# First block's attention: PE's order laid down by the source, scores of both heads in turns and two steps ahead

## The chip, the cores and the metric

The kernel runs on one core of one Trainium2 chip. The metric is the time of one execution on the device, in microseconds (us); of several runs the median is given. The profile is of one execution.

The engines of the core are called as the profile calls them: PE (TensorE; its matmuls, with PEld for the weight loads that run beside them), DVE (VectorE), ACT (ScalarE), POOL (GpSimd) and SP (SyncE, which issues most of the DMAs). Each engine takes its instructions in the order in which they stand in its own list, and waits in front of one until the semaphores that it names have been raised.

## The reference

A chain of three blocks, each on a sequence of 1024 rows of width 1024 in float32. The change is in the first. Its attention is a stick-breaking attention: no softmax over a row, but a running sum along the keys from the right.

```python
def stick_breaking_attention(q, k, v):
    scale = ATT_HEAD_DIM ** -0.5
    outs = []
    for blk in range(S // Q_BLOCK):          # Q_BLOCK = 128
        q0, q1 = blk * Q_BLOCK, (blk + 1) * Q_BLOCK
        z = einsum('bthd,bshd->bhts', q[:, q0:q1], k[:, :q1]) * scale
        log_fail = where(causal, log_sigmoid(-z), 0.0)
        later = cumsum(log_fail, axis=3, reverse=True) - log_fail
        w = where(causal, exp(log_sigmoid(z) + later), 0.0)
        outs.append(einsum('bhts,bshd->bthd', w, v[:, :q1]))
```

There are 8 heads of width 64 and 8 query blocks. The same block also has a gate for each of its two branches (`g_att`, `g_conv`, dense projections of the input), and a branch with a convolution of 31 taps and a layer norm. The second and third blocks follow with an average-pooling mixer, a banded attention, and a state-space layer.

## The kernel before

Dense products are made in three matmuls: each operand is split into a high and a low part, and hi·hi, hi·lo and lo·hi are added up (`mm3`, L156). Half of an output tile, 128 x 512, takes 8 blocks of depth x 3 = 24 matmuls; this text calls it a half dense. The split of a weight is a cast by ACT (`whi`, L146) and a subtraction by POOL (`wlo`, L147).

The attention of the first block walks over four pairs of heads, p = 0 to 3. The two heads of a pair lie in the same tiles `qh, ql, kh, kl`, head 0 in rows 0 to 63, head 1 in rows 64 to 127. For each pair there are eight steps, one for each query block tb (ascending for p = 0 to 2, descending for p = 3). A step, `attention_step`, does for each head:

- scores: three matmuls (qh·kh, qh·kl, ql·kh, L754) per bank `aux`, of which there are two; up to 512 keys make one part, more keys two parts; on the diagonal block a mask is added by a fourth matmul of 128 columns (L756); ACT copies the bank to `z` (L757)
- the chain on `z` and `e`: a minimum on DVE (L758), exponential and logarithm on ACT (L218), a maximum (L761), a scan from the right (L762) and a subtraction (L763) on DVE, an exponential on ACT (L218)
- transposes: pieces of 128 x 128 (L770), up to four to a bank `tp`, of which there are two; a step with more than four blocks (tb of 4 or more) needs two pieces for each head; a copy of each piece to `wt`, by ACT for head 0 (L773) and by DVE for head 1 (L775)

and then for both heads together the values (L783): per key block one matmul for each head, into one bank `o`, which four steps share; after the fourth, DVE multiplies the bank by a gate (`zt`, L707).

Between the steps the source calls the dense work that fills PE: gates after steps 1, 2, 3 and 6, the projections of the next pair's k and q after steps 4 and 5. Each piece of the convolution branch (`conv_branch`, 28 pieces, `K.bg`) is called behind a half dense, two at a time (`K.rate = 2`).

None of this is the order in which the engines run. A scheduler lays each engine's list by the dependences and by priority: the steps stand inside `high_priority(offset=2000)`, so an instruction of a step comes as soon as its operands may be there by the scheduler's estimate, and the dense work falls into the rest. Where `K.after(a, b)` is called, a stands behind b on its engine, without a semaphore.

## Time and profile before

| | |
|---|---|
| median of 3 runs | 3230.51 us (3230.08 to 3234.98) |
| the profiled execution | 3232.07 us |
| its span, from the first to the last instruction | 3230.3 us |
| mean granted TensorE clock | 0.978 |
| busy share of the span | PE 96%, PEld 77%, DVE 64%, POOL 43%, ACT 38% |
| the chain of work that ended last | PE 32%, of it 24% dense (L156); DVE 8%; DMA 3% |

"Busy" is the time in which an engine had an instruction under way. Matmuls overlap at their ends, so the durations of single ones add up to more than the time that passes; the distance from start to start is the cost. A row of the timeline shows the start, the time to the end of the last one of the row, and in brackets how long the engine had stood idle before it and what ended that. The clock is the share of full speed that was granted.

### The profile page before, as it was taken

The page shows a single profiled execution, that of the slowest core. Times are in us where ns is not written, and L with a number is a line of the kernel's source. Part 1 is how long each engine was busy: PE and PEld are TensorE (multiplying, and loading weights), DVE is VectorE, ACT ScalarE, POOL GpSimd, SP SyncE. Part 2 cuts the span into 40 slices and gives each one's busy share as a digit, 9 for nine tenths or more (in the row PEclk, how much of TensorE's full clock was granted, in tenths as well). Part 3 has the DMA queues.
Part 4 walks back from the last instruction along what each step waited for, and adds up shares of the span by engine and source line. Part 5 has one row for each costly group of instructions (what it writes and reads, how often), then busy time and mean ns, then how long its engine had stood idle before and what let it go on. Part 6 is the DMA issues. An engine that isn't in the chain of part 4 may idle for free. (4 is left out here: it accounts for less than half of the span.)

```text
span 3230.3 us, 41367 instructions
## 1 busy us (share of the span) xinstructions
PE 3106.3 (96%) x15397; PEld 2479.5 (77%) x15401; DVE 2052.8 (64%) x3302; ACT 1215.6 (38%) x2294; POOL 1376.0 (43%) x1065
## 2 busy tenths in 40 slices
PE   9999999999989999999999999999989989989997
PEld 7877677778777888777777777778778778778886
DVE  8986886663685364232268767784886887663444
ACT  3025555563252111111144344441114655743443
POOL 2323332214645344777744322342213553474455
PEclk9999999999989999999999999999999999989998
DMA  4132222134321112222212111337344232375322
GB/s 130 52 108 79 72 68 80 46 125 134 124 63 49 57 53 66 70 76 75 66 56 63 46 34 37 122 127 198 97 142 136 92 104 66 124 237 180 118 91 98
DMA packets 159737, 303.92 MB, mean 94 GB/s; under 512 B 23840, under 2 KB 66864, under 8 KB 159536
## 3 DMA queue, kind: packets, MB, share of 16 engines
q1 hardware_dynamic: 149104, 294.96, 28.8%
q10 hardware_dynamic: 10368, 6.30, 0.9%
q8 instruction: 121, 1.98, 0.3%
q14 instruction: 80, 0.66, 0.1%
q0 software_dynamic: 64, 0.03, 0.0%
HBM read 236.59 MB, written 64.62 MB: 93 GB/s over the span
## 5 line engine op out<-in xcount | busy, mean ns | idle before, releaser
L147 POOL TENSOR_TENSOR wlo<-wraw,whi 128x1024 fp32r<-128x1024 f32 (+1 forms) x305 | 750.6, 2462 | 1086.9 <-ACT whi L146 1049.4
L146 ACT CAST whi<-wraw 128x1024 fp32r<-128x1024 f32 (+1 forms) x309 | 308.2, 998 | 795.1 <-PE mm L156 588.7
L568 DVE SCALAR_TENSOR_TENSOR co<-cpad,conv_w,co 128x1024 f32<-128x1024 f32 x120 | 179.7, 1537 | 0.9
L1640 DVE SCALAR_TENSOR_TENSOR h<-cp,conv_w,h 128x512 f32<-128x512 f32 x96 | 90.6, 943 | 20.0 <-ACT h L1638 19.0
L156 PE MATMUL mm<-mixh,whi 128*128 128x512 f32 x256 | 99.3, 393 | 2.9 <-DVE h L927 2.0
L156 PE MATMUL mm<-mixh,wlo 128*128 128x512 f32 x256 | 99.8, 391 | 0.0
L156 PE MATMUL mm<-mixl,whi 128*128 128x512 f32 x256 | 99.7, 391 | 0.0
L218 ACT ACTIVATE e<-e 128x128 f32<-128x128 f32 (+7 forms) x128 | 84.5, 681 | 33.5 <-DVE e L758 32.6
L762 DVE TENSOR_TENSOR_SCAN e<-e 128x128 f32<-128x128 f32 (+7 forms) x64 | 93.9, 1475 | 0.7
L927 DVE TENSOR_TENSOR h<-h,mm 128x512 f32<-128x512 f32 x64 | 43.3, 680 | 59.4 <-PE mm L156 59.3
L761 DVE TENSOR_TENSOR e<-e,z 128x128 f32<-128x128 f32 (+7 forms) x64 | 53.8, 850 | 37.1 <-ACT e L218 37.0
L320 DVE TENSOR_TENSOR sq<-sq,sq 128x512 f32<-128x512 f32 (+1 forms) x46 | 53.8, 1170 | 29.7 <-ACT sq L319 28.7
L218 ACT ACTIVATE z<-z 128x128 f32<-128x128 f32 (+7 forms) x64 | 43.3, 683 | 76.6 <-DVE z L763 76.5
L1958 DVE TENSOR_TENSOR h<-h,mm 128x512 f32<-128x512 f32 x32 | 21.9, 685 | 78.3 <-PE mm L156 78.3
L832 DVE TENSOR_TENSOR sz<-mm,row 128x512 f32<-128x512 f32 x32 | 22.0, 689 | 75.1 <-PE mm L156 75.1
L319 ACT ACTIVATE sq<-h 128x512 f32<-128x512 f32 x60 | 37.7, 629 | 73.4 <-POOL h L1990 29.7
L156 PE MATMUL mm<-y00h,whi 128*128 128x512 f32 x146 | 59.7, 410 | 3.9 <-DVE zt L1797 3.2
L916 DVE TENSOR_TENSOR cv<-mm,cv 128x512 f32<-128x512 f32 x16 | 11.1, 692 | 81.4 <-PE mm L156 81.4
L156 PE MATMUL mm<-y01h,whi 128*128 128x512 f32 x146 | 58.7, 403 | 3.3 <-ACT y01h L68 2.5
L156 PEld LDWEIGHTS mm<-mixh,whi 128*128 128x128 f32 x256 | 48.0, 188 | 15.5 <-issue 3.1
L156 PE MATMUL mm<-y30l,whi 128*128 128x512 f32 x146 | 58.0, 397 | 2.0 <-DVE y30l L71 2.0
L156 PE MATMUL mm<-y01l,whi 128*128 128x512 f32 x146 | 59.2, 406 | 0.2 <-DVE y01l L71 0.2
(1433 smaller groups left out, 10229.1 us busy)
## 6 DMA issues: line engine op xcount, KB each, us to landing
wraw<-w_in SPq DMA_DIRECT2D x76, 512.0 KB, 3.7
wraw<-w_in_even SPq DMA_DIRECT2D x53, 512.0 KB, 3.6
wraw<-w_in_odd SPq DMA_DIRECT2D x22, 512.0 KB, 3.6
sp_g<-gt SPq DMA_DIRECT2D x32, 256.0 KB, 2.0
g<-sp_g SPq DMA_DIRECT2D x32, 256.0 KB, 3.3
wraw<-w_out SPq DMA_DIRECT2D x16, 512.0 KB, 3.5
wraw<-w_out_even SPq DMA_DIRECT2D x32, 256.0 KB, 2.6
wraw<-w_out_odd SPq DMA_DIRECT2D x16, 512.0 KB, 3.6
```

The source lines that it names most:

```text
L146: self.nc.scalar.copy(hi, src)
L147: (eng or self.nc.gpsimd).tensor_sub(lo, src, hi.bitcast(F32))
L156: ins = self.nc.tensor.matmul(ps, a[:, k, :], b[:, cols], start=first and n == 0, stop=last and n == total - 1).ins
L218: ins = self.nc.scalar.activation(out, in_, func, **kw).ins
L319: nc.scalar.activation(sq, src, AF.Square, scale=scale)
L320: (nc.vector if self.count > 5 else self.engines[i]).tensor_add(self.accs[i], self.accs[i], sq)
L568: nc.vector.scalar_tensor_tensor(o, cpad[:, tap:tap + S], cw[:, j, tap:tap + 1], o, op0=ALU.mult, op1=ALU.add)
L761: nc.vector.tensor_tensor(e[:, :L], e[:, :L], z[:, :L], op=ALU.max)
L762: nc.vector.tensor_tensor_scan(e[:, rev], e[:, rev], e[:, rev], 0.0, op0=ALU.add, op1=ALU.bypass)
L832: nc.vector.tensor_mul(t, ps, row[hf])
L927: nc.vector.tensor_add(h[e][:, half(hf)], h[e][:, half(hf)], ps)
L1640: nc.vector.scalar_tensor_tensor(oh, c(d), cw[:, ch, 3 - d:4 - d], oh, op0=ALU.mult, op1=ALU.add)
```

## The change

`attention_step` becomes a class, `Attention1`, with the step cut in four: `open` (its tiles), `scores(s, part)`, `turn` (the transposes) and `values_of`. Steps are numbered through, s = 8p + n. Its parts are called in this order around the dense work: values of step s - 1, transposes of step s, first part of the scores of step s + 2, then a half dense. The second part of the scores comes between two half denses, or, where a step has one half dense only, in the middle of it (`K.within`, behind block 3 of 8). The dense work is handed out by halves: for p < 3 one half each of the next k and q after steps 0 to 3, a whole gate after steps 4 to 7; for p = 3 one half of a gate after each step.

The scores of the two heads take turns (kh·qh of head 0, of head 1, then the next product). The transposes of the two heads take turns by pieces. `K.queue` ties each of these PE instructions, and each dense matmul from then on, behind the one queued before it: PE's order in this stage is that of the source. At the start, the scores of steps 0 and 1 stand behind half 0 of k and q, and half 1 of both behind these.

The operations, their operands and shapes are the same in both kernels.

```diff
@@ mm3
-                ins = self.nc.tensor.matmul(ps, a[:, k, :], b[:, cols], ...).ins
+                ins = self.queue(self.nc.tensor.matmul(ps, a[:, k, :], b[:, cols], ...)).ins
...
+            if self.within and k == x.n // 2 - 1:
+                self.within, step = None, self.within
+                step()
@@
+    def queue(self, step):
+        if self.queued:
+            if self.tail is not None:
+                self.after(step.ins, self.tail)
+            self.tail = step.ins
+        return step
@@ attention of the first block
-    project("k", 0)
-    project("q", 0)
+    steps = Attention1(K, pb, v, mask, qk)
+    (k0, k1), (q0, q1) = by_halves(lambda: project("k", 0)), by_halves(lambda: project("q", 0))
+    k0()
+    q0()
+    K.queued = True
+    with K.tc.high_priority(offset=2000):
+        for s in range(2):
+            steps.open(s)
+            steps.scores(s, 0)
+    k1()
+    q1()
     K.bg += conv_branch(K, pb)
...
+        fill = []
         if p < 3:
-            fill[4] = lambda: project("k", p + 1)
-            fill[5] = lambda: project("q", p + 1)
+            fill += [[r] for name in "kq" for r in by_halves(lambda name=name: project(name, p + 1))]
+        gates = [r for i in range(4) for r in by_halves(lambda i=i: gate(4 * p + i))]
+        fill += [gates[2 * i:2 * i + 2] for i in range(4)] if p < 3 else [[r] for r in gates]
         for n in range(8):
+            s = 8 * p + n
             with K.tc.high_priority(offset=2000):
-                o = attention_step(K, pb, p, tb, qh, ql, kh, kl, v, mask, o if n % 4 else None)
...
-            if n in fill:
-                fill[n]()
+                steps.values_of(s - 1)
+                steps.turn(s)
+                if s + 2 < 32:
+                    steps.open(s + 2)
+                    steps.scores(s + 2, 0)
+            def more(s=s):
+                with K.tc.high_priority(offset=2000):
+                    steps.scores(s + 2, 1)
+            if s + 2 < 32 and len(fill[n]) == 1:
+                K.within = more
+            fill[n][0]()
+            if len(fill[n]) == 2:
+                more()
+                fill[n][1]()
+    K.queued, K.tail = False, None
+    steps.values_of(31)
     K.drain()
@@ class Attention1, scores
+        banks = [K.aux_bank() for _ in range(2)]
+        for i, (a, b) in enumerate(((qh, kh), (qh, kl), (ql, kh))):
+            for hh, ps in enumerate(banks):
+                rows = slice(hh * 64, hh * 64 + 64)
+                K.queue(nc.tensor.matmul(ps[:, :n], a[rows, ts], b[rows, c0:c0 + n], ...))
+        if diag:
+            for ps in banks:
+                K.queue(nc.tensor.matmul(ps[:, n - 128:n], K.identb, self.mask, start=False, stop=True))
@@ class Attention1, turn
         for s0 in range(0, tb + 1, 4):
             ns = min(4, tb + 1 - s0)
+            for hh, (z, wt) in enumerate(zip(zs, wts)):
+                pt = K.tp_bank()
+                for i in range(ns):
+                    K.queue(nc.tensor.transpose(pt[:, i * 128:(i + 1) * 128], z[:, ...], K.ident))
```

Lines move: the dense matmul from L156 to L157, the scores from L754 to L807, the mask from L756 to L810, the copy to `z` from L757 to L812, minimum, maximum, scan and subtraction from L758, L761, L762, L763 to L816, L819, L820, L821, the transposes from L770 to L834, the copies to `wt` from L773 and L775 to L837 and L839, the values from L783 to L853, `zt` from L707 to L859, ACT's exponentials from L218 to L222.

Three places follow, all in the third pair of heads (p = 2), around the steps tb = 4 to 6, as the engines' lists have them. In brackets stands what an instruction waits for: a semaphore of PE, of ACT (Activation), of DVE, of POOL or of a DMA queue. Numbers behind a name tell tiles apart.

PE before, at the scores of step tb = 6: `aux_759` is the second part of head 0, with the mask, and `aux_765` the first part of head 1.

```order
L754 MATMUL aux_759_4831<-kh_573_3735,qh_596_3875 128x384 [waits PE_49]
L754 MATMUL aux_759_4831<-kl_574_3736,qh_596_3875 128x384
L754 MATMUL aux_759_4831<-kh_573_3735,ql_597_3876 128x384
L756 LDWEIGHTS identb_239
L756 MATMUL aux_759_4831<-attmaskb_241,identb_239 128x128
L754 MATMUL aux_765_4858<-kh_573_3735,qh_596_3875 128x512 [waits Activation_49]
L754 MATMUL aux_765_4858<-kl_574_3736,qh_596_3875 128x512
L754 MATMUL aux_765_4858<-kh_573_3735,ql_597_3876 128x512
L156 MATMUL mm_707_4519<-x01l_25_189,whi_702_4485 128x512
L156 MATMUL mm_707_4519<-x01h_24_188,wlo_703_4486 128x512
```

PE after, at the same step: `aux_729` is the first part of head 0, `aux_730` that of head 1.

```order
L807 MATMUL aux_729_4594<-kh_505_3335,qh_543_3522 128x512
L807 MATMUL aux_730_4595<-kh_505_3335,qh_543_3522 128x512
L807 MATMUL aux_729_4594<-kl_506_3336,qh_543_3522 128x512
L807 MATMUL aux_730_4595<-kl_506_3336,qh_543_3522 128x512
L807 MATMUL aux_729_4594<-kh_505_3335,ql_544_3523 128x512
L807 MATMUL aux_730_4595<-kh_505_3335,ql_544_3523 128x512
L157 MATMUL mm_734_4610<-x00h_8_130,whi_732_4605 128x512
L157 MATMUL mm_734_4610<-x00l_9_131,whi_732_4605 128x512
L157 MATMUL mm_734_4610<-x00h_8_130,wlo_733_4606 128x512 [waits Pool_49]
```

Before, the three matmuls of one head's bank stand together; after, those of the two heads take turns, ahead of the dense work.

PE before, at the transposes of step tb = 4, head 1 (`z_716`): one piece of four blocks into `tp_721`, one of a single block into `tp_722`.

```order
L754 MATMUL aux_743_4722<-kh_573_3735,qh_596_3875 128x384 [waits Activation_49]
L754 MATMUL aux_743_4722<-kl_574_3736,qh_596_3875 128x384
L770 MATMUL tp_721_4598<-ident_235,z_716_4577 128x128 [waits Activation_49]
L770 MATMUL tp_721_4598<-ident_235,z_716_4577 128x128 x3
L770 MATMUL tp_722_4604<-ident_235,z_716_4577 128x128
L754 MATMUL aux_743_4722<-kh_573_3735,ql_597_3876 128x384
L756 LDWEIGHTS identb_239
L756 MATMUL aux_743_4722<-attmaskb_241,identb_239 128x128
L156 MATMUL mm_704_4490<-x20l_13_146,whi_702_4485 128x512
```

PE after, at the transposes of the same step (`z_688` is head 0, `z_689` head 1).

```order
L853 MATMUL mm_671_4303<-wt_703_4474,v_242 64x128
L853 MATMUL mm_671_4303<-wt_704_4475,v_242 64x128
L834 MATMUL tp_721_4572<-ident_235,z_688_4391 128x128 [waits PE_49,Activation_49]
L834 MATMUL tp_721_4572<-ident_235,z_688_4391 128x128 x3
L834 MATMUL tp_722_4578<-ident_235,z_689_4392 128x128 [waits PE_49,Activation_49]
L834 MATMUL tp_722_4578<-ident_235,z_689_4392 128x128 x3
L834 MATMUL tp_723_4584<-ident_235,z_688_4391 128x128 [waits Activation_49]
L834 MATMUL tp_724_4587<-ident_235,z_689_4392 128x128 [waits DVE_49]
```

Before, the two pieces of a head stand between scores, with one wait; after, the four pieces of both heads stand behind the values of the step before, the first two waiting for `z` (ACT) and their banks, the third for ACT, the fourth for DVE.

DVE before, in the same stretch: `wt_720` takes head 1 of step tb = 4, `e_734` and `e_741` are the two heads of step tb = 5.

```order
L758 TENSOR_SCALAR e_734_4685<-z_733_4684 128x768 [waits Activation_49]
L761 TENSOR_TENSOR e_734_4685<-e_734_4685,z_733_4684 128x768 [waits Activation_49]
L762 SCALAR_TENSOR_TENSOR e_734_4685<-e_734_4685 128x768 [waits DVE_49]
L763 TENSOR_TENSOR z_733_4684<-z_733_4684,e_734_4685 128x768 [waits DVE_49]
L775 COPY wt_720_4597<-tp_721_4598 128x512 [waits PE_49]
L775 COPY wt_720_4597<-tp_722_4604 128x128 [waits PE_49]
L758 TENSOR_SCALAR e_741_4716<-z_740_4715 128x768 [waits Activation_49]
L761 TENSOR_TENSOR e_741_4716<-e_741_4716,z_740_4715 128x768 [waits Activation_49]
L762 SCALAR_TENSOR_TENSOR e_741_4716<-e_741_4716 128x768 [waits DVE_49]
```

DVE after: `wt_720` is again head 1 of step tb = 4, `e_709` and `e_710` the two heads of step tb = 5, `zt_717` the product with the bank of values of steps tb = 0 to 3.

```order
L816 TENSOR_SCALAR e_709_4490<-z_707_4488 128x768 [waits Activation_49]
L816 TENSOR_SCALAR e_710_4491<-z_708_4489 128x768 [waits Activation_49]
L819 TENSOR_TENSOR e_709_4490<-e_709_4490,z_707_4488 128x768 [waits Activation_49]
L859 TENSOR_TENSOR zt_717_4565<-mm_671_4303,zt_717_4565 128x512 [waits DMAHW7_49,DMAHW1_49,PE_49]
L820 SCALAR_TENSOR_TENSOR e_709_4490<-e_709_4490 128x768 [waits DVE_49]
L839 COPY wt_720_4571<-tp_722_4578 128x512 [waits PE_49]
L819 TENSOR_TENSOR e_710_4491<-e_710_4491,z_708_4489 128x768 [waits Activation_49]
L821 TENSOR_TENSOR z_707_4488<-z_707_4488,e_709_4490 128x768 [waits DVE_49]
L839 COPY wt_720_4571<-tp_724_4587 128x128 [waits PE_49]
L820 SCALAR_TENSOR_TENSOR e_710_4491<-e_710_4491 128x768 [waits DVE_49]
```

Before, both copies to `wt_720` stand together between the chains of two heads; after, the first stands behind the product with `zt` and a scan, and the second behind a maximum and a subtraction more.

## Rows read from the trace of the kernel before

**Rows 1.** Stretches of the stage, all engines: the stretch and its length, busy time of each engine (x instructions), the mean granted clock, the share of the DMA engines and what they moved.

```profile
264.00:370.00 106.00, 98.94 (x537) 73.95 (x538) 91.33 (x137) 62.41 (x118) 35.33 (x28) 0.95 0.19 61
370.00:480.00 110.00, 102.80 (x542) 76.25 (x537) 95.69 (x132) 60.36 (x116) 37.03 (x28) 0.97 0.24 81
480.00:600.00 120.00, 120.00 (x657) 91.10 (x657) 84.68 (x111) 66.89 (x118) 36.51 (x26) 1.00 0.20 67
600.00:712.00 112.00, 110.09 (x599) 81.98 (x598) 71.24 (x90) 67.42 (x118) 18.09 (x7) 0.94 0.24 85
264.00:712.00 448.00, 431.82 (x2326) 323.27 (x2326) 342.93 (x468) 257.08 (x469) 126.97 (x88) 0.97 0.22 73
```

The busy times are in the order PE, PEld, DVE, ACT, POOL.

**Rows 2.** The same stretch, PE alone and one line of the kernel at a time, in this order: scores (L754), masks (L756), transposes (L770), values (L783). Busy time (x instructions), clock, DMA.

```profile
264.00:712.00 448.00, 75.26 (x288) 0.97 0.22 73
...
264.00:712.00 448.00, 14.89 (x64) 0.97 0.22 73
...
264.00:712.00 448.00, 44.05 (x288) 0.97 0.22 73
...
264.00:712.00 448.00, 50.72 (x576) 0.97 0.22 73
```

**Rows 3.** PE's timeline at the scores of a step of the first pair, two banks of 512 columns: start, us, line, operation, tiles and shapes.

```profile
338.80 0.50 PE L754 MATMUL aux<-kh,qh 64*128 64x512 f32 x1
339.14 0.39 PE L754 MATMUL aux<-kl,qh 64*128 64x512 f32 x1
339.37 0.39 PE L754 MATMUL aux<-kh,ql 64*128 64x512 f32 x1
...
340.38 0.23 PE L756 MATMUL aux<-attmaskb,identb 128*128 128x128 bf16 x1
340.42 0.48 PE L156 MATMUL mm<-x20h,whi 128*128 128x512 f32 x1
```

**Rows 4.** PE's timeline in the attention of the second block, where heads in the lower and the upper 64 rows alternate.

```profile
1788.15 0.38 PE L1082 MATMUL aux<-kh,qh 64*128 64x256 f32 x1
1788.16 0.38 PE L1082 MATMUL stat<-kh,ql 64*128 64x256 f32 x1
1788.37 0.28 PE L1082 MATMUL aux<-kl,qh 64*128 64x256 f32 x1
1788.38 0.28 PE L1082 MATMUL stat<-kh,qh 64*128 64x256 f32 x1
1788.49 0.28 PE L1082 MATMUL aux<-kh,ql 64*128 64x256 f32 x1
```

**Rows 5.** PE's timeline at five of its stops in the stage; in brackets the idle time before and what ended it.

```profile
268.93 0.44 PE L754 MATMUL aux<-kh,qh 64*128 64x384 f32 x1 [1.87 <-ACT z L757]
...
350.88 0.76 PE L281 MATMUL stat<-ones,sq 128*128 128x1 f32 x4 [2.86 <-DVE sq L324]
...
352.08 0.63 PE L156 MATMUL mm<-x21h,wlo 128*128 128x512 f32 x1
352.51 0.63 PE L156 MATMUL mm<-x31h,whi 128*128 128x512 f32 x1
...
450.37 0.50 PE L754 MATMUL aux<-kh,qh 64*128 64x512 f32 x1 [2.07 <-ACT z L757]
...
457.05 1.52 PE L783 MATMUL mm<-wt,v 128*64 128x128 f32 x22 [1.36 <-DVE wt L775]
458.51 0.76 PE L770 MATMUL tp<-ident,z 128*128 128x128 f32 x5
...
473.77 2.59 PE L783 MATMUL mm<-wt,v 128*64 128x128 f32 x24 [3.13 <-DVE wt L775]
```

**Rows 6.** Groups of DVE's instructions from 242 to 712 us, by shape: xcount, busy time, mean ns of one, idle time before and what ended it.

```profile
L648 DVE RECIPROCAL lnsum<-lnsum 128x256 f32<-128x256 f32 x16 | 27.9, 1744 | 0.3
...
L762 DVE TENSOR_TENSOR_SCAN e<-e 128x768 f32<-128x768 f32 x8 | 17.2, 2147 | 0.1
...
L775 DVE COPY wt<-tp 128x512 f32<-128x512 f32 x24 | 16.0, 682 | 8.9 <-PE tp L770 8.9
...
L761 DVE TENSOR_TENSOR e<-e,z 128x768 f32<-128x768 f32 x8 | 8.0, 997 | 7.8 <-ACT e L218 7.8
...
L758 DVE TENSOR_SCALAR e<-z 128x768 f32<-128x768 f32 x8 | 5.0, 619 | 2.3 <-ACT z L757 2.3
L707 DVE TENSOR_TENSOR zt<-mm,zt 128x512 f32<-128x512 f32 x7 | 4.6, 664 | 7.3 <-PE mm L783 7.3
```

**Rows 7.** Groups of ACT's instructions from 242 to 712 us, by shape.

```profile
L757 ACT COPY z<-aux 128x512 f32<-128x512 f32 x32 | 18.0, 586 | 6.4 <-PE aux L756 4.7 <-PE aux L754 1.7
L218 ACT ACTIVATE e<-e 128x1024 f32<-128x1024 f32 x16 | 16.9, 1058 | 8.1 <-DVE e L758 8.0
...
L773 ACT COPY wt<-tp 128x512 f32<-128x512 f32 x24 | 13.6, 581 | 6.1 <-PE tp L770 5.9
```

**Rows 8.** The timelines of ACT and POOL where half 0 of q of the first pair is split.

```profile
258.26 0.69 ACT L673 ACTIVATE qkf<-mm,b 128x512 f32<-128x512 f32 x1 [3.38 <-PE mm L156]
258.99 0.62 ACT L146 CAST qh<-qkf 128x512 fp32r<-128x512 f32 x1
...
259.69 1.28 POOL L147 TENSOR_TENSOR ql<-qkf,qh 128x512 fp32r<-128x512 f32 x1 [2.33 <-ACT qh L146]
```

More of the change, by code (lines that the diff above doesn't have):

```diff
@@ L155, in mm3 @@
             for a, b in ((hi, xh), (hi, xl), (lo, xh)):
-                ins = self.nc.tensor.matmul(ps, a[:, k, :], b[:, cols], start=first and n == 0, stop=last and n == total - 1).ins
+                ins = self.queue(self.nc.tensor.matmul(ps, a[:, k, :], b[:, cols], start=first and n == 0, stop=last and n == total - 1)).ins
                 if self.pin is not None:
@@ L667, in project, with ev @@
         qk[name, p] = (hi, lo)
-        def ev(_, hf, ps):
+        def ev(hf, ps):
             hs = half(hf)
@@ L684, in ev, with by_halves, run @@
             spilled(K, "g", i, half(hf), t)
-        K.dense([w_in[28 + i]], x, ev)
-    project("k", 0)
-    project("q", 0)
+        return w_in[28 + i], ev
+    def by_halves(make):
+        made = []
+        def run(hf):
+            if hf == 0:
+                src, ev = make()
+                made.extend([K.weight(src, 8, 128), ev])
+            K.one(made[0], x, hf, made[1])
+        return [lambda: run(0), lambda: run(1)]
+    steps = Attention1(K, pb, v, mask, qk)
+    (k0, k1), (q0, q1) = by_halves(lambda: project("k", 0)), by_halves(lambda: project("q", 0))
@@ L776, in attention_step @@
-        wts.append(wt)
-    if o is None:
-        o = K.mm_bank()
-    oc = slice((tb % 4) * 128, (tb % 4) * 128 + 128)
-    for sb in range(tb + 1):
-        for hh in range(2):
-            hd = 2 * p + hh
-            nc.tensor.matmul(o[hh * 64:hh * 64 + 64, oc], v[:, sb, hd * 64:hd * 64 + 64], wts[hh][:, sb, :],
-                             start=sb == 0, stop=sb == tb)
-    return o
+            for hh, (z, wt) in enumerate(zip(zs, wts)):
+                pt = K.tp_bank()
+                for i in range(ns):
+                    K.queue(nc.tensor.transpose(pt[:, i * 128:(i + 1) * 128], z[:, (s0 + i) * 128:(s0 + i + 1) * 128], K.ident))
+                src = pt[:, :ns * 128].rearrange("p (a b) -> p a b", b=128)
+                if hh == 0:
+                    nc.scalar.copy(wt[:, s0:s0 + ns, :], src)
+                else:
+                    nc.vector.tensor_copy(wt[:, s0:s0 + ns, :], src)
@@ new lines, in values_of @@
+    def values_of(self, s):
+        if s < 0:
+            return
+        K, nc, pb, (p, tb), n = self.K, self.K.nc, self.pb, self.at(s), s % 8
+        wts = self.wt.pop(s)
+        if n % 4 == 0:
+            self.o = K.mm_bank()
+        oc = slice((tb % 4) * 128, (tb % 4) * 128 + 128)
+        for sb in range(tb + 1):
+            for hh in range(2):
+                hd = 2 * p + hh
+                K.queue(nc.tensor.matmul(self.o[hh * 64:hh * 64 + 64, oc], self.v[:, sb, hd * 64:hd * 64 + 64], wts[hh][:, sb, :],
+                                         start=sb == 0, stop=sb == tb))
+        if n % 4 == 3:
+            hs = half(tb // 4)
+            zt = pb.tile([128, HALF], F32, tag="zt", name=K.n("zt"), bufs=1)
+            nc.sync.dma_start(zt, K.spill["za", p][:, hs])
+            nc.vector.tensor_mul(zt, self.o, zt)
+            if p < 3:
+                spilled(K, "az", p, hs, zt)
+            else:
+                self.late.append((tb // 4, zt))
```

94 lines of the change are left out of this document (43 added, 51 removed).

## The prediction

> **What bounds the kernel now.** I read the clock and the span first, then the stretches of the stage by engine, then the groups of PE instructions in it, then PE's timeline where it stands still, and last the groups of VectorE and ScalarE.
>
> The stretches [rows 1] show the first block's attention from 264 to 712 us: 448 us, in which PE is busy 431.8. The four rows above the last are roughly the head pairs p = 0 to 3. So PE is the bound, and little idle time is left: 448 - 431.8 = 16.2 us. The last column group adds a second loss: the granted clock is 0.97 in the mean. VectorE is busy 342.9 us of the same 448, and in the first two pairs 91.3 of 106 and 95.7 of 110. It is the next engine in line, and close.
>
> Of PE's time the attention proper is [rows 2]: scores 75.3 us, masks 14.9, transposes 44.1, values 50.7; the dense projections, whose number does not change, fill the rest. Neighbours overlap in these busy times, so they are upper ends.
>
> PE's stops are few and have causes that can be read [rows 5]: 1.87 and 2.07 us before scores, which waited for ScalarE to empty their bank (ACT z), 1.36 and 3.13 before values, which waited for VectorE's copy of the weights (DVE wt), 2.86 before a sum of the convolution branch. After such a stop the chip grants half the clock, the 1.2 GHz level: behind the stop at 350.88 the dense matmuls start 0.43 us apart (352.08 to 352.51) instead of the 0.23 of [rows 3]. Two rows of values show the same: 22 in 1.52 us after 1.36 of idling, 24 in 2.59 after 3.13. I put the half-clock stretches of the stage at 9 us beyond their work, by counting the wide intervals, and so the removable loss at 16 + 9 = 25 us.
>
> **The change, part by part.** The instructions are the same ones. What changes is where they stand, and which of them stand side by side.
>
> *Scores, both heads in turns.* Before, six matmuls of 512 columns run from 338.80 to 340.38: two heads one behind the other, 0.26 us each [rows 3]. They use 64 of 128 rows each, head 0 the lower and head 1 the upper. In the second block's attention, where matmuls of 256 columns with 64 rows alternate, two start 10 ns apart and the next two some 0.1 to 0.2 us later [rows 4]: such a pair costs as much as one. In the new order all 288 alternate (first place of the order rows). Half of 75.3 is 38; the busy time of 85 short runs counts some overlap, so I take -33. The ends are 0 (they do not run together) and -38.
>
> *Masks.* 64 matmuls, 14.9 us busy. A mask with a dense matmul behind it costs 0.04 us (340.38 to 340.42 [rows 3]). Now the two of a step stand together behind the scores: -5, ends 0 and -9.
>
> *Values.* 22 of them from 457.05 to 458.51 are 1.46 us, 0.13 a pair [rows 5]; 288 pairs in unbroken runs are 38 to 40 us instead of 50.7: -11, ends -5 and -13.
>
> *Fewer changes of kind.* By count of the order, PE goes through 364 stretches of one kind before and 210 after. A first matmul of a kind costs about 0.1 us more than its successors (0.34 against 0.23 [rows 3]): 154 x 0.1 = 15, about half of it already in the terms above. With transposes in longer runs: -8, ends -4 and -15.
>
> *The old stops and their half clock* go, because the order that made them is gone: -25. Without any new stop the stage would be 448 - 33 - 5 - 11 - 8 - 25 = 366 us.
>
> That number is the first warning. VectorE's 343 us would be 94% of it, in an engine that takes its work in order and shares chains with PE and ScalarE. Something must wait, and PE's order being fixed, PE waits where the order says, without other work to step in. I price the waits that can be seen in the order.
>
> *First scores.* The scores of steps 0 and 1 now follow half 0 of q directly, where before the other half stood between. PE must see ScalarE add the bias and cast, and POOL make the low part: 0.69 + 0.62 + 1.28 [rows 8] = 2.6, with the hand-overs +3. With less to do in between than I think, 1.3 (the first scores need the high part alone).
>
> *Transposes in steps of more than four blocks* (tb of 4 or more, 16 steps). Before, one head's pieces stood at a time, at most two, with dense work around them (second place). Now four pieces of both heads stand in one go for two PSUM banks, and the third and fourth need a bank just filled. In 12 steps they wait for ScalarE's copies: two copies of 0.58 us at most [rows 7] less the 0.4 us of the other head's transposes, with hand-overs some 1.3 us each: 12 x 1.3 = 16. If ScalarE stands in an exponential of 1.06 us at the time [rows 7], 2.4.
>
> In the four steps with tb = 4 the fourth piece waits for VectorE, and there VectorE's order decides (third place): the copy stands behind the zt product, which itself waits for PE's values just ahead of the transposes, and behind a scan: 0.66 + 2.15 + 0.68 = 3.5 us [rows 6], less about 1 us of transposes meanwhile. That is 2.5 if VectorE is otherwise up to date. If two minima (0.62 each) and a maximum (1.00) are still to do as well, it is 4.7, and with a RECIPROCAL of the convolution branch (1.74) 6.5. For p = 0 and 1, where VectorE is 0.86 busy, I take 6.7, for p = 2 3.4, and for p = 3 1.2 (no zt stands there): 18.
>
> Behind such a wait stands everything on PE: the scores of the next step but one, the dense half, and so in turn VectorE's own next chain.
>
> *Other waits.* At one step of the last pair ScalarE's copy stands behind the exponential of the following step, which waits for a whole scan and subtraction: +4. The sums of the convolution branch keep their place in the order, with VectorE's work now in blocks of two heads ahead of them; 2.86 before [rows 5], 6 each at two places: +12, ends 4 and 16.
>
> So new waits 16 + 18 + 4 + 12 = 50. Of these about eight are longer than 3 us, and each brings a stretch at half clock of the kind after 350.88, some 1.8 us: +14, ends 6 and 25.
>
> **Sum.** 366 + 3 + 50 + 14 = 433 against 448: -15 us. The profiled execution took 3232.07 (span 3230.3 plus 1.8 around it), the new one would take 3217. The median of the runs shown is 1.6 lower, so 3215.5; I say 3216. Three later places of the program are also ordered a little differently (the way into the second block, into its second layer, and the end of the third block); no work is added there, and I give them nothing, with 3 us either way.
>
> **A rule weighed.** The ScalarE copies of a 512-wide score bank take 0.59 us each [rows 7]; a pair of heads fills two banks in about 0.8 us (half of 1.58 [rows 3]) where it took 1.6, and emptying both takes 1.17. So by the rows the emptying becomes slower than the filling, but 12 or 24 dense matmuls (2.7 or 5.5 us at 0.23) lie between two fillings, and hide it. The Trainium skill, "TensorEngine Tiling (Array Packing)", section "PSUM Bottleneck", says that packing the array speeds up the matmuls but not the emptying of PSUM, and that the copies may become the limit. By that rule the transposes rather than the scores are the place to fear, since nothing lies between their fillings; its result is the second rival below.
>
> **Rivals.** (a) *The waits mostly vanish.* Scores come two steps ahead, so the weights of a step have about 26 us of PE time to get ready, and VectorE's backlog may be worked off in it; with 10 to 15 us of waits and clock instead of 67, the stage is 366 + 13 = 379, which VectorE would fill to 0.9. With some of its own waiting I put it at 393: -55, 3176. For it: the long slack. Against it: the copies are tied to the moment of the transposes, not to slack, and VectorE's 0.9.
>
> (b) *Slower: PE and VectorE go in lockstep.* All 16 large steps wait as the tb = 4 steps do, since ScalarE and VectorE are both in a two-head block of the softmax chain when the transposes come: 4 us each, 64 instead of 34, and half clock behind each of the 16, hardly less than 1 us each. That is +30 at the same clock loss, the stage is 463: 3231 + 15 = 3246. It decides from about 3.1 us a step on (34 + 15 over 16). For it: VectorE's share, and its order at the third place. Against it: in 12 of the 16 steps the wait is for a ScalarE copy only, and ScalarE was busy 257 of 448 us [rows 1].
>
> (c) *The alternating heads do not run together here*, and the change doesn't do what it says: 33 us come back, 3216 + 33 = 3249. Against it are [rows 4]; there the two tiles of a pair lie in two banks, as here.
>
> (d) *The gain is just eaten*: a few of the sizes above at their upper ends (12 x 2.4 instead of 1.3 is +13 alone), no difference.
>
> **How the numbers follow.** 0.2% is 6.5 us, about what a measurement of this kernel can tell from no change. The forecast as such (3203 to 3224) 0.44, (a) 0.18, (b) 0.20, (c) 0.05, (d) 0.13. Faster: 0.41 of the first, and (a) with 0.18: 0.59. Same: 0.03 of the first, 0.12 of (d), 0.03 of (b): 0.18. Slower: the rest of (b) and (c), and 0.01 of (d): 0.23. The range takes in the middle of (a) and nearly all of (b): 3176 to 3249; the forecast's own range is 3203 to 3224.
>
> **What would show it.** In the new profile: the scores' busy time in the stage near 40 to 45 us, with starts of the two heads some 10 ns apart. PE waiting at the third and fourth transpose piece of the large steps, near 1.3 us for ScalarE and at tb = 4 up to 6.7 for VectorE's copy. No stop before scores for ACT z except the first of about 3 us. VectorE at 0.79 of a stage of 433 us instead of 0.77. The mean granted clock of the stage still near 0.96. It is wrong if the scores stay near 75 us, if the stops at the transposes are all below 0.5 us, or if they are 4 us each.

## The result and the profile after

The changed kernel takes 3256.28 us (median of 4 runs, 3253.38 to 3259.74) against 3230.3 beside it: ratio 1.0077, 95% interval 1.0061 to 1.0093. It is slower by 0.8%, where 0.5% faster was forecast.

Nearly all of it arises in the stage, the part of the first block with the attention. Counted from 242 us to the last matmul of the values, it lasted until 710.5 us in the kernel before and until 733.8 in the changed one, 23.3 of the 25.7 us between the two profiled executions:

```profile
242.00:710.50 468.50, 452.46 (x2418) 340.29 (x2416) 344.59 (x470) 263.84 (x477) 135.57 (x93) 0.97 0.22 74
```

That is the kernel before, stretches with all engines (PE, PEld, DVE, ACT, POOL, clock, DMA); the same view of the changed kernel, with the stretches of [rows 1] ahead of the whole:

```profile
264.00:370.00 106.00, 88.16 (x472) 66.67 (x471) 83.06 (x110) 59.05 (x104) 40.16 (x25) 0.90 0.18 60
370.00:480.00 110.00, 93.23 (x532) 70.46 (x531) 88.74 (x124) 53.99 (x102) 43.69 (x34) 0.94 0.23 76
480.00:600.00 120.00, 102.76 (x573) 78.13 (x573) 84.66 (x109) 59.60 (x110) 36.01 (x23) 0.90 0.18 61
...
242.00:733.80 491.80, 424.43 (x2405) 323.16 (x2406) 356.10 (x474) 263.73 (x477) 142.36 (x92) 0.92 0.21 71
```

PE has 28.0 us less to do (452.5 to 424.4) and stands still 51.3 us longer (468.5 - 452.5 = 16.0 to 491.8 - 424.4 = 67.4). The clock falls from 0.97 to 0.92. In the third stretch, where PE had not been idle at all, it now is for 17 of 120 us. VectorE's share falls from 0.74 to 0.72: it is not full. But it is busy for 356.1 us instead of 344.6 with the same instructions; e5 below comes back to that.

PE's time by line, in the order of [rows 2] (scores, masks, transposes, values), one line each:

```profile
242.00:734.00 492.00, 45.83 (x288) 0.92 0.21 71
...
242.00:734.00 492.00, 9.98 (x64) 0.92 0.21 71
...
242.00:734.00 492.00, 48.32 (x288) 0.92 0.21 71
...
242.00:734.00 492.00, 39.68 (x576) 0.92 0.21 71
```

So the matmuls did become cheaper, the scores by 29 us. Where PE stands is in its groups (x, busy, mean, idle before and what ended it):

```profile
L834 PE MATMUL tp<-ident,z 128*128 128x128 f32 x288 | 48.3, 298 | 39.9 <-ACT wt L837 29.9 <-DVE wt L839 10.1
L853 PE MATMUL mm<-wt,v 128*64 128x128 f32 x576 | 39.8, 279 | 2.6 <-DVE wt L839 2.6
L807 PE MATMUL aux<-kh,qh 64*128 64x384 f32 (+3 forms) x96 | 25.3, 493 | 10.4 <-ACT z L812 9.4 <-ACT qh L147 1.0
```

39.9 of the 67.4 us are waits of transposes for a copy out of a transpose bank. PE's timeline at step tb = 4 of the first pair:

```profile
310.15 1.09 PE L853 MATMUL mm<-wt,v 128*64 128x128 f32 x16
311.18 1.09 PE L834 MATMUL tp<-ident,z 128*128 128x128 f32 x8
316.04 0.33 PE L834 MATMUL tp<-ident,z 128*128 128x128 f32 x1 [3.77 <-ACT wt L837]
320.24 0.48 PE L834 MATMUL tp<-ident,z 128*128 128x128 f32 x1 [3.86 <-DVE wt L839]
320.64 0.80 PE L807 MATMUL aux<-kh,qh 64*128 64x512 f32 x2
321.23 0.63 PE L807 MATMUL aux<-kl,qh 64*128 64x512 f32 x2
```

The first two pieces (eight transposes) fill both banks at once; the third stands 3.8 us, the fourth 3.9, and behind it the products of the scores start 0.59 us apart where 0.33 is seen elsewhere (339.49 to 339.82 in e1 below). The granted clock from 320.64 to 322.20 is 0.50, the 1.2 GHz level. What ScalarE did meanwhile:

```profile
310.13 0.84 ACT L812 COPY z<-aux 128x384 f32<-128x384 f32 x2
311.54 1.72 ACT L222 ACTIVATE e<-e 128x768 f32<-128x768 f32 x2 [0.57 <-DVE e L816]
313.17 1.03 ACT L147 CAST whi<-wraw 128x1024 fp32r<-128x1024 f32 x1
314.10 0.68 ACT L685 ACTIVATE qkf<-mm,b 128x512 f32<-128x512 f32 x1
314.68 0.83 ACT L222 ACTIVATE e<-e 128x768 f32<-128x768 f32 x1
315.41 0.57 ACT L837 COPY wt<-tp 128x512 f32<-128x512 f32 x1
```

The copy that PE waits for could have started at about 311.7, when the first four transposes were through (an estimate, half of the row at 311.18). In ScalarE's list it stands behind two exponentials and a logarithm of the next step (`e<-e`), a weight's cast and the evacuation of a projection, and runs at 315.41. VectorE's copy likewise:

```profile
314.90 2.43 DVE L656 TENSOR_SCALAR lnsum<-lnt 128x256 f32<-128x256 f32 x1
317.26 0.68 DVE L859 TENSOR_TENSOR zt<-mm,zt 128x512 f32<-128x512 f32 x1
317.86 1.74 DVE L820 TENSOR_TENSOR_SCAN e<-e 128x768 f32<-128x768 f32 x1
319.52 0.66 DVE L839 COPY wt<-tp 128x512 f32<-128x512 f32 x1
```

It stands behind a piece of the convolution branch, the zt product and a scan; the last two the order had shown. The first takes 2.43 us here; in e5 instructions of its line and shape take 0.50 in the mean. At tb = 4 the two waits together are 9.4 us for p = 1 and 4.5 for p = 2; for p = 3 there is one wait of 4.8, for ScalarE.

The waits before scores have a longer chain behind them. Rows of VectorE, POOL, ScalarE and PE ahead of the first long one:

```profile
286.56 4.48 DVE L820 TENSOR_TENSOR_SCAN e<-e 128x512 f32<-128x512 f32 x2
...
286.91 3.05 POOL L148 TENSOR_TENSOR wlo<-wraw,whi 128x1024 fp32r<-128x1024 f32 x1 [3.58 <-ACT whi L147]
...
291.66 1.23 ACT L222 ACTIVATE z<-z 128x512 f32<-128x512 f32 x2 [3.94 <-DVE z L821]
292.80 0.60 ACT L147 CAST kh<-qkf 128x512 fp32r<-128x512 f32 x1
293.31 0.85 ACT L812 COPY z<-aux 128x384 f32<-128x384 f32 x2
...
293.83 0.96 PE L807 MATMUL aux<-kh,qh 64*128 64x256 f32 x2 [3.00 <-ACT z L812]
```

Of the two scans the first takes 1.22 us and the second, beside POOL's subtraction, 3.34. ScalarE stands idle for 3.94 us in front of an exponential that needs the scan's result, and the copy that empties the score banks stands behind it. The wait of 4.62 us at 554.37 has the same rows ahead of it, with a scan of 3.33 us.

### The profile page after: what moved, and what is told of

Same layout as the page of the kernel before. It is cut to its first block, busy times and chain, and to the rows that moved or that the text cites. A ratio compares the mean times of both kernels' runs of the same rounds, so it can differ in the third digit from the quotient of the medians.

```text
span 3256.0 us, 41364 instructions
## 1 busy us (share of the span) xinstructions
PE 3078.0 (95%) x15397; PEld 2460.4 (76%) x15401; DVE 2062.2 (63%) x3302; ACT 1217.4 (37%) x2294; POOL 1377.2 (42%) x1065
## 5 line engine op out<-in xcount | busy, mean ns | idle before, releaser
L820 DVE TENSOR_TENSOR_SCAN e<-e 128x128 f32<-128x128 f32 (+7 forms) x64 | 105.7, 1675 | 0.1
L157 PE MATMUL mm<-mixh,whi 128*128 128x512 f32 x256 | 99.4, 393 | 2.7 <-DVE h L1005 1.8
L157 PE MATMUL mm<-mixh,wlo 128*128 128x512 f32 x256 | 99.8, 391 | 0.0
L157 PE MATMUL mm<-mixl,whi 128*128 128x512 f32 x256 | 99.7, 391 | 0.0
L222 ACT ACTIVATE e<-e 128x256 f32<-128x256 f32 (+7 forms) x128 | 79.6, 674 | 22.9 <-DVE e L816 22.5
L834 PE MATMUL tp<-ident,z 128*128 128x128 f32 x288 | 48.3, 298 | 39.9 <-ACT wt L837 29.9
L222 ACT ACTIVATE z<-z 128x128 f32<-128x128 f32 (+7 forms) x64 | 43.2, 685 | 94.2 <-DVE z L821 94.2
L834 PEld LDWEIGHTS tp<-ident,z 128*128 128x128 f32 x288 | 32.6, 148 | 52.7 <-ACT wt L837 36.3
L819 DVE TENSOR_TENSOR e<-e,z 128x128 f32<-128x128 f32 (+7 forms) x64 | 48.0, 779 | 32.1 <-ACT e L222 32.1
L157 PE MATMUL mm<-y00h,whi 128*128 128x512 f32 x146 | 59.2, 406 | 4.5 <-DVE zt L1875 3.5
L157 PE MATMUL mm<-y01h,wlo 128*128 128x512 f32 x146 | 58.6, 401 | 3.2 <-POOL wlo L148 3.2
L157 PE MATMUL mm<-y01h,whi 128*128 128x512 f32 x146 | 58.6, 403 | 3.0 <-ACT y01h L68 2.2
```

The costliest lines, as they stand in the source:

```text
L157: ins = self.queue(self.nc.tensor.matmul(ps, a[:, k, :], b[:, cols], start=first and n == 0, stop=last and n == total - 1)).ins
L222: ins = self.nc.scalar.activation(out, in_, func, **kw).ins
L819: nc.vector.tensor_tensor(e[:, :L], e[:, :L], z[:, :L], op=ALU.max)
L820: nc.vector.tensor_tensor_scan(e[:, rev], e[:, rev], e[:, rev], 0.0, op0=ALU.add, op1=ALU.bypass)
L834: K.queue(nc.tensor.transpose(pt[:, i * 128:(i + 1) * 128], z[:, (s0 + i) * 128:(s0 + i + 1) * 128], K.ident))
```

## The experiments

Each kernel ran beside the kernel before. "Stage" is from 242 us to the last matmul of the values in the profiled execution; busy and idle are PE's in it. (Outside the stage the kernels differ by up to some 15 us from one list to another, so the ratio follows the stage only roughly.)

| kernel | median us | ratio to before (95%) | stage | PE busy | idle |
|---|---|---|---|---|---|
| before | 3230.3 to 3233.9 | 1 | 468.5 | 452.5 | 16.0 |
| changed | 3256.28 | 1.0077 (1.0061 to 1.0093) | 491.8 | 424.4 | 67.4 |
| e1 heads apart | 3256.27 | 1.0074 (1.0054 to 1.0093) | 492.2 | 424.0 | 68.2 |
| e2 turn split | 3252.0 | 1.0060 (1.0045 to 1.0075) | 481.9 | 425.0 | 56.9 |
| e3 order free | 3226.97 | 0.9979 (0.9970 to 0.9989) | 458.4 | 447.2 | 11.2 |
| e4 before, heads in turns | 3244.29 | 1.0034 (1.0022 to 1.0045) | 474.0 | 444.4 | 29.6 |
| e5 copies ahead | 3236.26 | 1.0008 (0.9995 to 1.0021) | 462.9 | 418.7 | 44.2 |
| e6 convolution behind | 3254.80 | 1.0069 (1.0054 to 1.0084) | 477.9 | 417.8 | 60.1 |
| e7 free, glued | 3224.69 | 0.9974 (0.9965 to 0.9984) | 453.7 | 438.8 | 14.9 |
| e8 turn free | 3233.37 | 0.9993 (0.9984 to 1.0003) | 462.2 | 427.5 | 34.7 |
| e9 mask between | 3262.26 | 1.0095 (1.0078 to 1.0112) | 493.4 | 446.1 | 47.3 |
| e10 both | 3259.15 | 1.0079 (1.0064 to 1.0094) | 494.8 | 443.9 | 50.9 |
| e11 transposes free | 3224.73 | 0.9979 (0.9967 to 0.9990) | 454.8 | 413.1 | 41.7 |
| e12 ahead, transposes free | 3261.11 | 1.0084 (1.0063 to 1.0105) | 494.9 | 433.9 | 61.0 |

**e1: the heads of a part one behind the other.**

```diff
-        for i, (a, b) in enumerate(((qh, kh), (qh, kl), (ql, kh))):
-            for hh, ps in enumerate(banks):
-                rows = slice(hh * 64, hh * 64 + 64)
+        for hh, ps in enumerate(banks):
+            rows = slice(hh * 64, hh * 64 + 64)
+            for i, (a, b) in enumerate(((qh, kh), (qh, kl), (ql, kh))):
```

> The changed kernel, but the three score matmuls of head 0 stand ahead of the three of head 1, not in turns. Theory A (PE's work still counts between its stops; pairing is worth what the traces show, 69.6 us of scores before and 42.7 after): 20 to 27 us slower than the changed kernel, about 3280 us, scores back near 70 us of PE time. Theory B (VectorE's and ScalarE's chains pace the stage, so PE time saved only turns into PE waiting): within 6 us of the changed kernel's 3256, with fewer us of PE idle instead.

The edit did not do what it was for, and that is a result. PE's list has head 0's three matmuls ahead of head 1's in all 48 parts, yet PE's timeline shows them side by side:

```profile
339.49 0.50 PE L807 MATMUL aux<-kh,qh 64*128 64x512 f32 x2
339.82 0.40 PE L807 MATMUL aux<-kl,qh 64*128 64x512 f32 x2
340.05 0.39 PE L807 MATMUL aux<-kh,ql 64*128 64x512 f32 x2
340.37 0.50 PE L157 MATMUL mm<-x00h,whi 128*128 128x512 f32 x1
```

Six matmuls of 512 columns in 0.88 us. That the stage is the same (492.2) says nothing on A or B. The pairing comes from standing next to each other, not from taking turns.

**e9: a mask between the heads.** As e1, with head 0's mask ahead of head 1's matmuls:

```diff
-        if diag:
-            for ps in banks:
+            if diag:
                 K.queue(nc.tensor.matmul(ps[:, n - 128:n], K.identb, self.mask, start=False, stop=True))
```

> The changed kernel with the scores head after head and, in the 32 parts with a mask, the mask of head 0 between the two heads' matmuls. e1_heads_apart showed that PE runs the two heads side by side even when they stand one behind the other; a mask uses all 128 rows and should keep them apart. Scores and masks rise from 46.6 us of PE time to about 62 (two thirds of the 27 us that pairing saved). If PE's time counts between its stops: the stage grows from 491.9 us to 505 to 511, the time to 3270 to 3275. If the stops absorb it (the copies come when they come): stage 487 to 497, 3250 to 3260, with less idle time before transposes.

This does part the heads, in the 32 parts with a mask: scores and masks take 71.7 us from start to start, more than the 62 expected. PE is busy 446.1 us instead of 424.4, 21.7 more, and idle 20.1 less; the stage grows by 1.6 us, and the median (3262.26) lies 2 us above the second range. So in the fixed order PE's time for the scores is not what counts: what pairing saves, PE spends waiting. But the waits that give way are not those before transposes, as was expected (38.9 us, before 39.9): 7.9 us go before scores, 8.7 before sums of the convolution branch, 2.6 before values.

**e2: the second transpose pieces elsewhere.**

```diff
-                steps.turn(s)
+                steps.turn(s, 0)
...
             def more(s=s):
                 with K.tc.high_priority(offset=2000):
+                    steps.turn(s, 1)
                     steps.scores(s + 2, 1)
```

> The changed kernel, but the second pieces of the transposes (tb of 4 or more) stand with the second part of the scores, behind or in the middle of the half dense, instead of right behind the first pieces. Theory A (the two transpose banks asked for four times in one go make PE wait 39.9 us, and the half clock behind these stops as much as 15 more): idle before transposes falls below 15 us and the time to 3205 to 3230. Theory B (VectorE and ScalarE are simply late; where PE asks does not matter): the idle time moves to other places, 3248 to 3264.

PE's groups:

```profile
L837 PE MATMUL tp<-ident,z 128*128 128x128 f32 x288 | 42.7, 281 | 7.2 <-DVE wt L842 6.9 <-ACT z L222 0.3
...
L808 PE MATMUL aux<-kh,qh 64*128 64x384 f32 (+3 forms) x96 | 31.3, 485 | 41.3 <-ACT z L813 40.2 <-ACT qh L147 1.0
```

The waits before transposes go, 39.9 to 7.2, as A said, but now the scores wait 40.2 us for ScalarE to empty their banks. The stage is 9.9 us shorter, and the time is in B's range. Two banks of one kind in a row are not the cause by themselves: whatever PE wants next from ScalarE comes late.

**e3: PE's order left to the scheduler**, with the same source: the line `K.queued = True` goes.

> The changed kernel without the chain that fixes PE's order; the source order, the pairs in the source and scores two steps ahead stay, the scheduler lays PE's list. Theory A (the fixed order is what makes PE wait): idle in the stage falls to 15 to 30 us, 3225 to 3245, with pairs mostly lost. Theory B: 3250 or more. A third theory C (asking for scores two steps ahead fills the few tiles of z and e and costs by itself): slower than the kernel before in any case, 3240 to 3260.

The stage shrinks by 33 us, below the kernel before; the time is in A's range, the idle time (11.2) below it. So asking for scores two steps ahead costs nothing by itself; C fell. What costs is PE's order as the ties fix it, together with the lists that the other engines then have: without the ties the scheduler lays those anew too (254 of ScalarE's 437 and 247 of VectorE's 441 instructions of the stage keep their relative order). Without the ties pairs are mostly lost (scores 63.6 us from start to start).

**e4: the kernel before, with heads in turns.** Scores of both heads part by part, and the six matmuls tied in that order.

> The kernel before, with the scores of both heads of a step emitted part by part in turns and the six matmuls of a part kept in that order; everything else, the scheduler's order too, stays. Theory A: scores fall from 69.6 us to 40 to 50, nothing else is lost, 3202 to 3215. Theory B (VectorE paces the stage): 3226 to 3236.

Scores fall from 69.6 to 53.1 us from start to start, idle rises by 13.6, values are more broken up: the stage is 5.5 us longer. Neither expectation held. That a pair can only start when the later of its two banks is empty may be part of it, but is not shown: idle before scores rises by 3.0 us only, before transposes by 5.1 and before values by 5.4.

**e5: the chain behind the copies.** PE's order as in the changed kernel; the chain of step s + 1 is issued after the transposes of step s and tied behind their copies on ScalarE and VectorE:

```diff
+            K.act(e[:, :L], e[:, :L], AF.Exp)
+            ex = K.users[-1]
+            if s >= 1:
+                K.after(ex, self.copied[0])
...
+            mx = nc.vector.tensor_tensor(e[:, :L], e[:, :L], z[:, :L], op=ALU.max).ins
+            if s >= 1:
+                K.after(mx, self.copied[1])
```

> The changed kernel with PE's order untouched, but the softmax chain of step s + 1 laid behind the transposes of step s on ScalarE and VectorE: its first exponentials stand behind ScalarE's copies to wt of step s, its maxima behind VectorE's. Theory A (the copies which PE waits for stand in their engine's list behind a chain that is itself late; in the changed kernel 26 waits for ScalarE's copy 29.9 us and 3 for VectorE's 10.1): the waits before transposes fall below 12 us together and the time to 3215 to 3238. Theory B (VectorE with ScalarE can not do a step's work in the time that PE leaves, wherever it stands): the waits turn into waits for the exponential z ahead of the transposes or for score banks, 3248 or more.

```profile
L847 PE MATMUL tp<-ident,z 128*128 128x128 f32 x288 | 48.9, 300 | 34.4 <-ACT z L222 27.7 <-ACT wt L850 4.2 <-DVE wt L852 2.0
...
L811 PE MATMUL aux<-kh,qh 64*128 64x384 f32 (+3 forms) x96 | 23.4, 471 | 1.7 <-ACT qh L147 1.0 <-ACT z L816 0.7
```

Of PE's list only the sums of the convolution branch stand elsewhere, and the stage is 29 us shorter: so what ScalarE's and VectorE's lists put ahead of the things that PE waits for makes a large part of the loss. The time is in A's range. Waits for copies fall from 39.9 to 6.2 us, which shows that it was the place in the list that made the copies late. But the waits before transposes as a whole fall only to 34.4, where A said below 12: 27.7 us of new waits for z come in, since the chain starts a step later and is not done when its transposes come. That is B's sign. Most of the gain lies elsewhere: 8.7 us less idle before scores, 6.5 before sums of the branch, 2.6 before values, and 5.7 less of PE's busy time.

Nor does VectorE take the same time for its work: it is busy 324.9 us instead of 356.1. The scans of 512 columns in the changed kernel and in e5:

```profile
L820 DVE TENSOR_TENSOR_SCAN e<-e 128x512 f32<-128x512 f32 x8 | 16.9, 2147 | 0.0
...
L833 DVE TENSOR_TENSOR_SCAN e<-e 128x512 f32<-128x512 f32 x8 | 10.7, 1343 | 0.0
```

The long ones run beside work of POOL, as at 286.56 above. How much of the 29 us is the order of the lists itself, and how much these longer instructions, was not parted. VectorE's time alone does not make the stage long: in e3 it is busy 356.5 us, in a stage of 458.4, so B in its strict form (the work does not fit) fell.

**e8: transposes and values out of the fixed order; e11: the transposes alone.** Their matmuls are no longer passed to `K.queue`.

> The changed kernel with transposes and values taken out of the fixed order; scores and dense matmuls keep theirs. Theory A (PE stands at transposes whose bank is not yet empty while dense work stands behind them): idle before transposes below 10 us, 3215 to 3238. Theory B: 3248 or more, with the waits at the scores, which still stand in the fixed order.

> The changed kernel with only the transposes out of PE's fixed order; scores, values and dense matmuls keep theirs. If it was the transposes' fixed place that made PE wait: idle below 30 us, with values still in unbroken runs (37 us of PE time against 48.3 in e8_turn_free), so the stage is shorter than that one's 462.3: 445 to 460, 3210 to 3230. If the wait only moves on to the values, which stand in the fixed order behind the same copies: stage 465 to 492, idle before values 15 us or more, 3232 to 3256.

The time of e8 lies in A's range (stage 462.2), though 21.7 us of idle before transposes are twice what A said, 12.1 of them for z, and values fall into pieces (53.1 us busy). e11 keeps these whole:

```profile
L834 PE MATMUL tp<-ident,z 128*128 128x128 f32 x288 | 50.6, 297 | 30.0 <-ACT z L222 12.0 <-ACT z L812 7.0 <-ACT wt L837 6.8
L853 PE MATMUL mm<-wt,v 128*64 128x128 f32 x576 | 38.9, 278 | 0.0
L807 PE MATMUL aux<-kh,qh 64*128 64x384 f32 (+3 forms) x96 | 25.0, 465 | 3.5 <-ACT z L812 2.5 <-ACT qh L147 1.0
```

Its stage is 37 us shorter than the changed kernel's and 13.7 shorter than before's. PE is busy least of all, and the wait did not move on to the values. Idle is above the 30 us expected, 41.7. Like e3 and e7 it is faster than both kernels, clear of 1 but by little (0.9979, 0.9979 and 0.9974 of the time before). Here too the other lists changed (326 of ScalarE's 437 and 296 of VectorE's 441 instructions keep their relative order), so the 37 us are those of the edit as a whole.

**e7: e3 with the six score matmuls tied in turns.**

> The kernel with the changed source order but PE's list laid by the scheduler (e3_order_free, 3227 us), and with the six score matmuls of a part kept in turns. If pairs are worth their PE time where PE does not wait: scores from 63.6 us to 45 to 50, 3208 to 3220. If glueing two banks together only makes the first matmul wait for the later bank, as in e4_before_heads_in_turns (16 us of PE time saved, 14 us of idle more): 3224 to 3240.

The glue brought 8 us of PE time and took 4 of idle: stage 453.7. Scores at 51.8 us from start to start missed the first expectation, and the median lies at the near edge of the second.

**e10 and e12: both repairs at once** (e5 with e8, e5 with e11).

> The changed kernel with both repairs: the chain of step s + 1 laid behind the copies of step s (e5_copies_ahead, 462.9 us for the stage) and transposes and values out of the fixed order (e8_turn_free, 462.3). If the copies' place and PE's fixed order are two sides of the same wait, the two add little: stage 452 to 465, 3222 to 3236. If they are separate, each worth 29 us: stage 435 to 450, 3205 to 3220.

> e5_copies_ahead with the transposes out of PE's fixed order, values kept in it. e10_both, with values out of it as well, came to 494.9 us for the stage with values at 53.4 us of PE time. If the values' broken runs were what spoilt e10_both: stage 445 to 465, values near 37 us, 3210 to 3236. If laying the chain behind the copies and leaving the transposes to the scheduler work against each other (the chain waits for copies that now come later): stage 470 or more, 3238 or more, with PE waiting for z (ACT) at transposes and at values.

Both are slow again, stage 494.8 and 494.9, outside both expectations of e10. In e12:

```profile
L847 PE MATMUL tp<-ident,z 128*128 128x128 f32 x288 | 47.4, 287 | 27.2 <-ACT z L222 19.6 <-DVE wt L852 5.8 <-ACT wt L850 1.5
L867 PE MATMUL mm<-wt,v 128*64 128x128 f32 x576 | 40.8, 283 | 4.0 <-ACT wt L850 4.0
L811 PE MATMUL aux<-kh,qh 64*128 64x384 f32 (+3 forms) x96 | 29.6, 458 | 27.4 <-ACT z L816 26.1 <-ACT qh L147 1.0
```

Values kept whole did not help. Stage and time are as in the second expectation of e12, and 19.6 us of waits for z stand before transposes; but values wait 4.0 us only, for copies, and most of the new idle time, 26.1 us, stands before scores, for ScalarE to empty their banks. That the chain, tied to copies which now come later, holds these up in ScalarE's list fits the rows; no run shows it by itself. In e10, with values free as well, less stands there (9.1 us) and values are broken up (56.7 us busy). Why two edits that bring 29 and 37 us bring nothing together stays open.

**e6: the convolution branch behind the attention** (`K.rate = 0`).

> The changed kernel with all 28 pieces of the convolution branch behind the attention instead of two behind each half dense. Theory B (VectorE's load makes it late, 81 us of the convolution's work among it): PE's idle time in the first two pairs of heads, about 40 us in the changed kernel, falls below 15, in the other two it stays. Theory A (the place of the copies in the lists decides): the stops at the steps with tb = 4 stay at 4 us or more in the first two pairs too. The total says little: VectorE's 81 us then stand alone, 3270 to 3320 by both.

Inconclusive for its question: the scheduler put the pieces into the stage all the same (VectorE busy 344.4 us from 242 to 720, 346.7 in the changed kernel). Whether the changed kernel's lists would fit without that work was not settled. The run shows something else: PE's list differs only in the place of the branch's sums, VectorE's in much more (314 of 441 keep their relative order), and the stage is 13.9 us shorter. The time is about the same (3254.80), since the rest of the program takes 11 us longer.

## Why the prediction was wrong

The terms, counted over all PE instructions of the stage from start to start, with idle taken out:

| term | forecast | before | after | measured |
|---|---|---|---|---|
| scores | -33 | 69.6 | 42.7 | -27.0 |
| masks | -5 | 6.1 | 3.9 | -2.2 |
| values | -11 | 46.6 | 37.3 | -9.3 |
| transposes, dense, sums of the branch | -8, and clock -9 + 14 | 330.0 | 340.5 | +10.5 |
| idle | -16 + 53 | 16.0 | 67.4 | +51.3 |
| stage | -15 | 468.5 | 491.8 | +23.3 |

Of the 38 us between forecast and result, 14 lie in the idle time, 13 in the row above it, 6 in the scores.

- *What bounds.* PE as the bound and VectorE as the next in line were read from [rows 1]. The first was right for the kernel before. For the changed one it is the wrong picture: e9 gives PE 22 us more to do and the stage grows by 2. VectorE's work was taken as a fixed 343 us; it took 356.1, and a share of 0.72 instead of the 0.79 named.
- *Scores.* The size was nearly right, the reading of [rows 3] was not: those six matmuls are the two parts of one head, in the same 64 rows, so they had to run one behind the other. What two heads do when they stand together was in [rows 4] alone. Neither the turns nor the order within a part matter (e1). The busy time by line, 75.3 to 45.8, is just above the 40 to 45 named.
- *Masks and values* were right in sign and within 3 us.
- *Fewer changes of kind, -8, with the clock at +5* is the first step that failed: +10.5 in its place. A stop costs more than its idle time. Dense matmuls at half-clock distance (0.38 to 0.7 us) rose from 31 to 81, and their loss over 0.227 each from 6.8 to 17.7 us, where +5 was put down for all of PE; the mean granted clock was 0.92, where 0.96 was named. The dense matmuls as a whole rose by 2.5 us only, so some 8 us were saved there as forecast (an estimate: 10.9 less 2.5). And transposes that wait restart one by one: they went from 37.9 to 45.7 us instead of falling. In 31 places one stands right ahead of idle time and takes 0.29 us, where one within a run takes 0.13.
- *Transposes in large steps.* Place and sum were right: 34 + 4 forecast, 39.9 measured. The parts were not. At tb = 4 the third piece also waits for ScalarE (3.8, 5.6 and 2.0 us for p = 0 to 2), which the order of ScalarE would have shown, and with the fourth the steps cost 7.6, 9.4 and 4.5 instead of 6.7, 6.7 and 3.4; for p = 3 the third piece costs 4.8, for ScalarE, where 1.2 was put down for VectorE. The first large step of p = 3 cost 5.3 (4 and 1.3 forecast), the others 0.6 to 0.9 instead of 1.3.
- *No stop before scores for ACT z* was wrong: 9.4 us at four places. 7.6 of it stands in two, where the copy stands in ScalarE's list behind an exponential that waits for VectorE (291.66 above). First scores cost 1.9 instead of 3; the sums of the branch 13.5 instead of 12, before 4.4.
- *The sum* is the second step that failed, and the deeper one. It took PE time saved and PE time waited as independent, and added them. In the fixed order what the matmuls save is given back as waiting (e9: 21.7 us more busy, 20.1 less idle), since what PE waits for comes when ScalarE's and VectorE's lists let it: with those lists in another order and PE's nearly the same, the stage is 29 us shorter (e5). With the ties off (e3), or off the transposes alone (e11), the same source is slightly faster than the kernel before.
- *Rivals.* The nearest time is that of (c), 3249, but its mechanism is excluded: the scores did fall from 75.3 to 45.8 us. Next is (b), 3246, and its place was right. Its mechanism as priced was not: the mean wait is 39.9/16 = 2.5 us a step, under the 3.1 from which it was to decide, and VectorE's share fell. The rest came from the half clock and the scores' waits. The result lies 7 us above the range.
- *The rule weighed.* The Trainium skill, "TensorEngine Tiling (Array Packing)", section "PSUM Bottleneck", names the emptying of PSUM as a possible limit once the array is packed. The trace agrees as to the place, 39.9 us of waits for such copies, but the copies themselves are short (0.57 us at 315.41); their place in the list makes them late. With another place (e5) 33.7 of the 39.9 us go, though waits for z take most of their room. That the scores' banks were safe behind half a dense output was wrong (9.4 us, and 40.2 in e2).

## What to carry to other kernels

When one engine's order is fixed by hand, look at the other engines' lists with it: what stands, in their order, ahead of each instruction that frees a buffer? A wait in a fixed list costs more than its idle time, since here the clock and restarts followed it, and work saved ahead of such a wait was worth next to nothing (e9). Here it paid to tie what must stay together (values, pairs of scores, dense runs) and to leave free what depends on late copies (the transposes alone: 37 us). Two such repairs need not add (e10, e12). And the busy time of an engine is not a constant of its instructions: sum it up anew for the changed kernel.

## What the hardware showed that was not expected

PE ran matmuls of two heads, in rows 0 to 63 and 64 to 127, at the same time although three matmuls of the first stood ahead of those of the second in its list (e1: six of 512 columns in 0.88 us). So PE does not start every matmul strictly in the order of its list, as the first section says of all engines. A mask, a matmul over all 128 rows, between them ends that (e9: scores from start to start 64.5 us instead of 42.7; the 16 parts without a mask still ran in pairs).

VectorE's scans took up to 2.8 times as long beside work of POOL: with 512 columns 1.2 to 3.4 us in the changed kernel. Of its 64 scans in the stage, 13 took over 1.2 times the shortest of their shape, all beside work of POOL; the 35 without any such work beside them are all short. Another 16 had some beside them and stayed short, so not every meeting costs.
